# The last ConvFFN's seven-product down projection, regrouped: where its pieces are split, which queue loads its weights, and the order of its last steps

## The chip, the cores and the metric

The kernel runs on one core of one Trainium2 chip. Its engines are TensorE (PE; PEld is its weight load), VectorE (DVE), ScalarE (ACT), GpSimd (POOL) and SyncE (SP). Each works through its own instructions in order and waits for others at semaphores. Transfers are issued from the queues of SyncE, POOL and ScalarE and run on 16 DMA engines. The metric is device microseconds (us) of one execution, as the median of several runs.

## What is computed

One inference step of a two-layer encoder trunk with 1,024 prompt frames and 32 frames of a running stream, model width 1,024. Each layer has a recurrent mixer (retention in layer 0, gated linear attention in layer 1) and a convolutional feed-forward block. The change touches that block of layer 1 and the final norm:

```python
def conv_ffn(h, conv_state, w_up, conv_w, conv_b, w_down):
    u = h @ w_up
    T = u.shape[1]
    ext = jnp.concatenate([conv_state.astype(u.dtype), u], axis=1)
    c = conv_b + ext[:, 0:T] * conv_w[0]
    for j in range(1, CONV_W):
        c = c + ext[:, j:j + T] * conv_w[j]
    gate, val = jnp.split(c, 2, axis=-1)
    return (jax.nn.silu(gate) * val) @ w_down, ext[:, T:]
...
        y, cs = conv_ffn(h, conv_states[i], ffn_w_up[i], ffn_conv_w[i], ffn_conv_b[i], ffn_w_down[i])
        new_conv.append(cs)
        x = x + y
    return rmsnorm(x, norm_final), ...
```

The inner width is 2,816, so `u` has 5,632 columns. All data are float32.

## The kernel before

**Number format.** A float32 operand is split into a high part (`hi`, a ScalarE cast) and a low part (`lo`, a VectorE subtraction of the cast from the raw value). A product is then three matmuls: hi x hi, hi x lo, lo x hi.

**Tokens.** T = 1,056 columns (1,024 + 32) in four quarters of TH = 264. A "half" s = 0 or 1 is two quarters; one matmul covers one quarter's width of 264.

**Up stage (`ffn_up`).** 22 units f, each one 128-row tile of the gate half and one of the value half. A 2x2 block product is done with seven block products instead of eight (`seven`): sums of the activations (made once) and of the weights (per unit) are multiplied, and sums of the results taken. So a unit is 7 products x 2 halves, each product 4 x 3 matmuls. Results go from PSUM through ScalarE copies (`snap`, line 415) and VectorE additions (`put`, line 1818) to a buffer `U[f]`. When a unit is through, `conv(f)` makes the convolution of both tiles: per tile two POOL copies into `cst`, one ScalarE activation (line 1844) and two VectorE instructions (1845, 1846), then a SiLU and the gate product (1869, 1870). In layer 1 `pair_sums` goes on: two units make a pair k = f // 2, and seven sums of the pair's blocks (line 1866) are stored as seven pieces in `scr_h7`.

**Down stage (`Down7`).** 11 pairs k against 4 pairs p of output tiles, again seven products m = 1, 2, 6, 5, 7, 4, 3 (`ORD`). It runs in steps n = 0 to 13: step n takes pairs n-3 to n (those that exist) against output pair p = (n + 1) % 4, so a step sums 1, 2, 3, 4, ... 4, 3, 2, 1 pairs: 44 in all. A step has 7 products i x 2 halves s, each 3 matmuls per pair; steps 3 to 10 have 168 matmuls, all steps 1,848.

- `load_x(k, i)` loads a raw piece on SyncE into one of 28 regions (four pairs held at a time; pair k overwrites pair k - 4, which was last used in the step before) and returns `split`, the cast (1627) and the subtraction (1628). Pairs 0 and 1 are loaded during the last up unit (`early`). From pair 4 on, piece i of pair n + 1 is loaded behind product i of step n, and a piece is cast when the list `late` holds more than two.
- `weights(n)` loads two raw weight blocks, `dg` and `dv`, on SyncE (1637), and makes seven operands from them: three splits (1641, 1642), four sums (1647 to 1649, 1654) and the split of `dwv` (1651, 1652). There are three raw tiles and ten tiles for operands; a step uses seven. So a load must wait until an earlier raw tile has been read for the last time.
- `product` takes results out of PSUM: ScalarE copies m = 1 (1685), 6 (1689), 7 (1692); VectorE adds 2 (1687), 5 to 7's copy (1693), 4 (1695), 3 (1698). The bank of m = 5 is accumulated on by m = 3, the last product, which so has to wait for line 1693. Output blocks of 528 come from two rings, five blocks for A and two for B, and are added to the residual `scr_x` in memory by accumulating transfers on POOL (1702).
- From step 10 on `settle` adds the products to the residual itself, which `fetch` has loaded into `Y` (additions at 1713), `squares` sums squares per quarter, and when the last output pair is through, `rms_row` (two matmuls `pn` with ones, line 231, and short ScalarE and VectorE steps, 243 to 250) and the lines 1749 and 1753 normalise a quarter and store it.

**What sets the order.** The program text gives priorities; a scheduler then places every instruction in its engine's order, one whose inputs it thinks late behind others. Engines keep that order on the chip. `order(a, b)` makes the scheduler place a behind b without a semaphore.

```python
                    if 2 <= n + 1 < len(self.win) and i == (2 if n > 2 else 0):
                        self.weights(n + 1)
...
                    elif 3 < k < NP:
                        late.append(self.load_x(k, i))
                    if len(late) > 2 or late and k >= NP:
                        late.pop(0)()
```

## Time and profile before

| what | value |
|---|---|
| median of 3 runs | 2818.47 us (2817.72 to 2820.93) |
| the profiled execution's own time | 2821.19 us |
| its span, first to last instruction | 2819.4 us |
| mean granted TensorE clock | 0.993 |
| first matmul of the down stage | 2542.0 us |
| transfers in the whole run | 379.90 MB, 135 GB/s on average |

A profile is one execution. Its span leaves out what lies ahead of the first and behind the last instruction. A row of a group of instructions reads: line, engine, operation, what it writes and reads, shapes and count, then busy time and mean duration, then idle time of that engine just before, with what ended it. A row of waits reads: who waited at which line, for whom, then us in total, times and the longest. A row of transfers reads: what, queue, count, KB each, median us from issue to landing. Matmul durations overlap, so the work of TensorE is best counted by matmuls per time.

### The profile page before, as it was taken

What the parts mean: (1) busy time and instruction counts of PE and PEld (TensorE: products, weight loads), DVE (VectorE), ACT (ScalarE), POOL (GpSimd) and SP (SyncE); (2) the same over time, 40 slices, a digit from 0 to 9 for tenths busy, and PEclk for the clock granted to TensorE, in tenths of its full rate; (3) what the DMA queues carried; (4) which work ended last, traced back from release to release, by engine and by line L of the source; (5) the groups of instructions that cost most, each with busy time, mean ns of one, the idle gap of its engine ahead of it and who ended that gap; (6) DMA issues with size and microseconds to landing.
All of it is one profiled execution on the core that took longest, in us unless ns stands there. A gap on an engine that the chain in (4) does not pass through costs nothing.

```text
span 2819.4 us, 54440 instructions
## 1 busy us (share of the span) xinstructions
PE 2762.1 (98%) x21954; PEld 2670.4 (95%) x21954; DVE 1989.9 (71%) x3450; ACT 1349.7 (48%) x2475; POOL 344.5 (12%) x628
## 2 busy tenths in 40 slices
PE   9999999999999999999999999999999999998997
PEld 9999988888999999999999999999999999998986
DVE  7876666667457877777555576764478888888657
ACT  7544454444345444444444466653354444455434
POOL 0000000000122111111000132210131111111112
PEclk9999999999999999999999999999999999999998
DMA  6333455554875222223755411116532332348772
GB/s 238 96 110 105 149 147 148 139 145 133 279 240 176 76 86 75 84 76 102 255 184 172 154 35 47 53 53 217 173 108 95 100 106 88 107 131 212 196 210 89
DMA packets 236158, 379.90 MB, mean 135 GB/s; under 512 B 58560, under 2 KB 162624, under 8 KB 232064
## 3 DMA queue, kind: packets, MB, share of 16 engines
q1 hardware_dynamic: 222864, 328.33, 36.0%
q0 software_dynamic: 12496, 47.54, 6.5%
q8 instruction: 172, 2.82, 0.4%
q14 instruction: 82, 0.67, 0.1%
q10 hardware_dynamic: 544, 0.54, 0.1%
HBM read 264.68 MB, written 111.67 MB: 133 GB/s over the span
## 4 chain that ended last, share of the span: by engine, by line
PE 80%; DVE 7%; ACT 3%; DMA 3%; issue 3%; POOL 2%; SPq 0%; DVEq 0%; ACTq 0%; POOLq 0%
PE pu L441 13%; PE pu L436 13%; PE pu L440 13%; PE pd L1519 5%; PE pd L1521 5%; PE pd L1520 5%; PE psv L270 2%; PE psv L271 2%; PE psv L272 2%; POOL x L1122 2%; PE pu L1676 2%; PE pu L1678 2%; PE pu L1679 2%; DMA raw<-w_ro 1%; DMA XA<-scr_h 1%
## 5 line engine op out<-in xcount | busy, mean ns | idle before, releaser
L110 DVE TENSOR_TENSOR wlo<-raw,whi 128x1024 fp32r<-128x1024 f32 x131 | 163.1, 1249 | 130.6 <-ACT whi L110 122.7
L415 ACT COPY HR<-pu 128x264 f32<-128x264 f32 x264 | 98.8, 375 | 302.5 <-PE pu L441 296.5
L110 ACT CAST whi<-raw 128x1024 fp32r<-128x1024 f32 x131 | 136.9, 1049 | 176.0 <-PE pd L1520 110.1
L441 PE MATMUL pu<-XA,wgl 128*128 128x264 f32 x752 | 213.4, 284 | 0.0
L436 PE MATMUL pu<-XA,wgh 128*128 128x264 f32 x752 | 212.8, 283 | 0.1
L440 PE MATMUL pu<-XA,wgh 128*128 128x264 f32 x752 | 212.6, 283 | 0.0
L1845 DVE SCALAR_TENSOR_TENSOR AR<-AR,cw 128x1058 f32<-128x1058 f32 x88 | 115.7, 1317 | 72.9 <-ACT AR L1844 71.4
L1818 DVE TENSOR_TENSOR AR<-HR,pu 128x264 f32<-128x264 f32 (+2 forms) x440 | 144.3, 367 | 3.0 <-PE pu L441 2.8
L1520 PE MATMUL pd<-hl,whi 128*128 128x384 f32 (+1 forms) x440 | 142.2, 323 | 0.1
L1519 PE MATMUL pd<-hh,whi 128*128 128x384 f32 (+1 forms) x440 | 142.2, 323 | 0.0
L1521 PE MATMUL pd<-hh,wlo 128*128 128x384 f32 (+1 forms) x440 | 141.8, 322 | 0.0
L436 PEld LDWEIGHTS pu<-XA,wgh 128*128 128x128 f32 x752 | 141.2, 188 | 0.3 <-ACT wgh L372 0.3
L440 PEld LDWEIGHTS pu<-XA,wgh 128*128 128x128 f32 x752 | 141.2, 188 | 0.0
L441 PEld LDWEIGHTS pu<-XA,wgl 128*128 128x128 f32 x752 | 141.1, 188 | 0.0
L436 PE MATMUL pu<-XA,wsh 128*128 128x264 f32 x464 | 132.5, 286 | 1.8 <-ACT HR L415 0.7
L373 DVE TENSOR_TENSOR wtl<-rv,wth 128x1024 fp32r<-128x1024 f32 x58 | 71.0, 1224 | 88.3 <-ACT wth L372 88.3
L441 PE MATMUL pu<-XA,wtl 128*128 128x264 f32 x464 | 131.9, 284 | 0.0
L441 PE MATMUL pu<-XA,wsl 128*128 128x264 f32 x464 | 131.8, 284 | 0.0
L436 PE MATMUL pu<-XA,wth 128*128 128x264 f32 x464 | 131.6, 284 | 0.0
L440 PE MATMUL pu<-XA,wsh 128*128 128x264 f32 x464 | 131.4, 283 | 0.0
L440 PE MATMUL pu<-XA,wth 128*128 128x264 f32 x464 | 131.1, 283 | 0.0
L1519 PE MATMUL pd<-XH,whi 128*128 128x264 f32 x432 | 123.6, 286 | 0.0
(604 smaller groups left out, 10529.5 us busy)
## 6 DMA issues: line engine op xcount, KB each, us to landing
raw<-w_down SPq DMA_DIRECT2D x60, 512.0 KB, 3.6
rg<-w_up SPq DMA_DIRECT2D x44, 512.0 KB, 3.5
rv<-w_up SPq DMA_DIRECT2D x44, 512.0 KB, 3.5
scr_h<-AR SPq DMA_DIRECT2D x77, 264.0 KB, 2.6
raw<-w_ro SPq DMA_DIRECT2D x39, 512.0 KB, 5.6
XH<-scr_hr POOLq DMA_DIRECT2D x16, 1056.0 KB, 7.1
scr_x<-AR POOLq DMA_DIRECT2D x60, 264.0 KB, 6.0
scr_h<-AR SPq DMA_DIRECT2D x22, 512.0 KB, 2.6
```

What stands on the lines that cost most here:

```text
L110: ins = S.copy(hi, raw), V.tensor_tensor(lo, raw, hi.bitcast(F32), op=ALU.subtract)
L270: PE.matmul(ps, ah, hi, start=kt == 0, stop=False)
L373: split_end[0] = split_last[0] = V.tensor_tensor(l_, src, h.bitcast(F32), op=ALU.subtract)
L415: ins = S.copy(t, b)
L436: mm = PE.matmul(ps, wh[:, k], x[:, 0, kt], start=m in (1, 2, 4, 5) and kt == 0, stop=False, skip_group_check=True)
L440: PE.matmul(ps, wh[:, k], x[:, 1, kt], start=False, stop=False, skip_group_check=True)
L441: mm = PE.matmul(ps, wl[:, k], x[:, 0, kt], start=False, stop=kt == 3, skip_group_check=True)
L1519: PE.matmul(o, w[0][:, k], h[0][:, :n], start=i == 0, stop=False)
L1520: PE.matmul(o, w[0][:, k], h[1][:, :n], start=False, stop=False)
L1521: self.last_mm = PE.matmul(o, w[1][:, k], h[0][:, :n], start=False, stop=i == nk - 1)
L1818: last_put[0] = V.tensor_tensor(u[:, d:d + n], t[:, o:o + n], b[:, o:o + n], op=op)
L1845: V.scalar_tensor_tensor(cj, uj[:, 1:T + 3], cw[:, nt, 1:2], cj, op0=ALU.mult, op1=ALU.add)
```

## The change

- **Pairs 0 and 1 are split in the up stage.** In units 5 to 18 `ahead_split` loads one stored piece back, casts it, subtracts, and stores high and low half to a new scratch `scr_h2`. `load_x` then loads both halves, twice the bytes, and nothing is split for these pairs in the down stage.
- **Late pieces are cast later**: when `late` holds more than three, behind a product of half 1, and placed behind that product's last matmul by `order`.
- **Weights** of step 3 on are loaded on POOL's queue instead of SyncE's. Those of steps 12 and 13 get homes in regions that pair 7 has left.
- **The last convolution** (unit 21) with its pair sums is called at step 2, and its two sums at steps 3, instead of ahead of the down stage; `o_conv` and the table load go with it. The buffers move by 8 columns for it.
- **A third block** in ring B, where the pre-split buffer `ready` was.
- **Steps 11 to 13 by half**: all of half 0 first, then all of half 1; the loads of `Y` and of these weights move into step 10 and to the start of step 11.

```diff
@@ Down7.__init__
-            self.blocks = [[HR[:, o * b:o * b + b] for o in range(3)] + [AR[:, o * b:o * b + b] for o in (8, 9)],
-                           [AR[:, o * b:o * b + b] for o in (10, 11)]]
+            self.blocks = [[HR[:, o * b:o * b + b] for o in range(3)] + [AR[:, 8 + o * b:8 + o * b + b] for o in (8, 9)],
+                           [AR[:, o:o + b] for o in (8 + 10 * b, 8 + 11 * b, 6 * b + 4)]]
@@ Down7.load_x
+            if k < 2:
+                nc.sync.dma_start(v.rearrange("p m j u -> p m (j u)").bitcast(F32), io["scr_h2"][k, :, i:i + n])
+                return None
...
-            def split():
-                S.copy(hi, raw)
+            def split(behind=None):
+                ins = S.copy(hi, raw)
+                if behind is not None:
+                    order(ins, behind)
                 V.tensor_tensor(lo, raw, hi.bitcast(F32), op=ALU.subtract)
@@ Down7.weights
-        def weights(self, n):
+        def weights(self, n, home=None, queue=nc.sync):
...
-                nc.sync.dma_start(r[:, :2 * h], io["w_down7"][o:o + 2 * h * P].rearrange("(p c) -> p c", p=P))
+                queue.dma_start(r[:, :2 * h], io["w_down7"][o:o + 2 * h * P].rearrange("(p c) -> p c", p=P))
@@ Down7.run
-        def run(self):
...
+        def run(self, last_conv):
+            N = len(self.win)
+            seq = [(n, s, i) for n in range(NP) for i in range(7) for s in range(2)]
+            seq += [(n, s, i) for s in range(2) for n in range(NP, N) for i in range(7)]
+            late, todo = [], []
+            for n, s, i in seq:
+                self.product(n, s, i)
+                k = n + 1
+                if s == 0:
+                    if n < NP - 2 and k > 1 and i == (2 if n > 2 else 0):
+                        self.weights(k, None, G if n > 1 else nc.sync)
+                    if n == NP - 2 and i == 2:
+                        self.weights(k, None, G)
+                        self.fetch(3)
+                    if n == NP - 1 and i in (1, 4):
+                        self.weights(NP if i == 1 else NP + 2, None if i == 1 else self.at[21][0][:, 20 * TH:], G)
+                    if n == NP - 1 and i in (1, 3, 5):
+                        self.fetch(i // 2)
+                    if n == NP and i == 0:
+                        self.weights(NP + 1, self.at[24][0], G)
+                    continue
+                if n >= NP:
+                    continue
+                if n == 2 and i == 1:
+                    todo = last_conv()
+                if todo and n > 2 and i in (2, 5):
+                    todo.pop(0)()
...
+                elif 3 < k < NP:
+                    late.append(self.load_x(k, i))
+                if len(late) > 3 or late and k >= NP:
+                    late.pop(0)(self.ends[n, s, i])
@@ ffn_up
+        def ahead_split(n):
+            k, i = divmod(n, 7)
+            raw, hi = ready[:, 2 * TH:], ready[:, :2 * TH]
+            nc.sync.dma_start(raw, io["scr_h7"][k, :, i].rearrange("p s t -> p (s t)"))
+            S.copy(hi.bitcast(F32R), raw)
+            V.tensor_tensor(raw.bitcast(F32R), raw, hi, op=ALU.subtract)
+            nc.sync.dma_start(io["scr_h2"][k, :, i], ready)
...
+                if he is not None and 4 < f < 19 and (s, i) == (1, 2):
+                    ahead_split(f - 5)
...
-                if s == 1 and i == 6:
+                if s == 1 and i == 6 and (he is None or f < NF - 1):
                     conv(f)
-            later(sums_h, 2)
+            if he is None:
+                nc.sync.dma_start(io["o_conv"][l], cst)
+
+        def last_conv():
+            conv(NF - 1)
             nc.sync.dma_start(io["o_conv"][l], cst)
+            ln_exp_table(last_silu[0])
+            return sums_h
```

94 lines of the change are left out of this document (39 added, 55 removed).

## The prediction

> **What bounds the kernel now.** I read the page's engine line first, then busy time by stretch, then the waits of each queue in the stretch that the change rewrites.
>
> ```profile
> span 2819.4 us, 54440 instructions
> PE 2762.1 (98%) x21954; PEld 2670.4 (95%) x21954; DVE 1989.9 (71%) x3450; ACT 1349.7 (48%) x2475; POOL 344.5 (12%) x628
> ```
>
> TensorE bounds the whole; only places where it waits can give time back. Busy time by stretch (each engine's busy us, its instructions in brackets, then granted clock, DMA share and GB/s):
>
> ```profile
> core 0: us, PE busy (x) PEld busy (x) DVE busy (x) ACT busy (x) POOL busy (x), PEclk, DMA share, GB/s
> 2441.50:2541.50 100.00, 100.00 (x826) 100.00 (x825) 84.15 (x132) 51.42 (x74) 13.02 (x32) 1.00 0.40 131
> 2541.50:2610.00 68.50, 58.60 (x450) 56.69 (x450) 59.10 (x99) 34.62 (x60) 14.46 (x19) 0.98 0.81 209
> 2610.00:2742.00 132.00, 125.08 (x990) 123.40 (x989) 83.31 (x137) 55.52 (x101) 19.11 (x23) 0.98 0.77 202
> 2742.00:2764.00 22.00, 22.00 (x178) 22.00 (x178) 12.51 (x26) 7.46 (x16) 4.15 (x6) 0.98 0.60 137
> 2764.00:2796.00 32.00, 31.23 (x254) 30.81 (x252) 24.32 (x57) 19.04 (x48) 13.95 (x19) 1.00 0.02 6
> 2796.00:2819.40 23.40, 4.40 (x8) 1.80 (x8) 18.76 (x42) 6.47 (x17) 0.00 (x0) 0.54 0.55 186
> ```
>
> The first row is the end of the up stage: 826 products in 100 us, 0.121 us each, and TensorE never waits. At that price the down rows lose 68.5 - 450 x 0.121 = 14.0 us (steps n = 0 to 3), 132 - 990 x 0.121 = 12.1 (n = 4 to 9), 0.4 (n = 10) and 1.2 (n = 11 to 13); then come 23.4 us with almost no products. These 51 us are all that the change can win. Who waits, from 2541 on:
>
> ```profile
> ACT XA L1627 <- DMA XA<-scr_h: 63.9, 21, 5.4
> DVE XA L1628 <- ACT XA L1627: 31.2, 15, 6.0
> ...
> ACT AR L1692 <- DMA scr_x<-AR: 13.8, 4, 5.2
> ...
> DVE dv L1647 <- DMA dv<-w_down: 11.0, 5, 2.9
> ...
> PE pu L1676 <- DVE AR L1693: 9.5, 9, 2.1
> ```
>
> and of SyncE's own queue:
>
> ```profile
> SPq L1637 <- DVE dwsl L1642: 25.8, 7, 9.4
> ```
>
> (us in total, times, longest). This reads as one chain: on SyncE a weight load waits until VectorE has freed its raw tile; the piece loads queued behind it start late; ScalarE stands in a cast (L1627) whose data have not landed; VectorE stands in the subtraction behind that; the addition L1693 is queued behind the subtraction, and the last product of the step needs the bank that L1693 reads. The wait costs more than itself, because TensorE's clock is lower after it:
>
> ```profile
> 2736.50:2739.00 2.50, 0.71 (x6) 0.50 (x5) 1.93 (x4) 1.74 (x3) 0.00 (x0) 1.00 0.67 209
> 2739.00:2742.50 3.50, 3.47 (x18) 3.48 (x19) 3.35 (x7) 2.19 (x5) 0.94 (x2) 0.59 0.28 74
> ```
>
> After some 2 us without a product the granted clock is 0.59 for 3.5 us, 1.4 us more lost.
>
> **A: steps 0 to 3, -6 us.** The 14 pieces of pairs 0 and 1 are no longer split here, and the last convolution is put further back. The built order of VectorE shows, though, that its convolution instructions still stand inside steps 0 and 1, and its product in step 2. So VectorE, 59.1 of 68.5 us busy now, stays the bound here. I count its instructions in the changed order from the end of the up stage to the second L1693-type addition of step 2: 57. Durations (busy us and mean ns behind the first bar; a shape has one duration whatever its tile):
>
> ```profile
> L1628 DVE TENSOR_TENSOR XA<-XA 128x1056 fp32r<-128x1056 f32 x4 | 5.0, 1249 | 0.0
> L1628 DVE TENSOR_TENSOR XA<-XA 128x528 fp32r<-128x528 f32 x34 | 23.7, 704 | 31.3 <-ACT XA L1627 31.2
> L1642 DVE TENSOR_TENSOR dwtl<-dv,dwth 128x1024 fp32r<-128x1024 f32 x8 | 9.8, 1223 | 1.2 <-ACT dwth L1641 1.2
> L1642 DVE TENSOR_TENSOR dwtl<-dv,dwth 128x768 fp32r<-128x768 f32 x2 | 1.9, 954 | 0.1
> L1654 DVE TENSOR_TENSOR dv<-dv,dg 128x512 f32<-128x512 f32 x8 | 5.5, 690 | 0.2
> L1654 DVE TENSOR_TENSOR dv<-dv,dg 128x384 f32<-128x384 f32 x2 | 1.1, 555 | 0.0
> L1693 DVE TENSOR_TENSOR AR<-AR,pu 128x264 f32<-128x264 f32 x20 | 8.3, 422 | 0.8 <-ACT AR L1692 0.8
> L1845 DVE SCALAR_TENSOR_TENSOR AR<-AR,cw 128x1058 f32<-128x1058 f32 x2 | 2.6, 1314 | 0.0
> L1844 ACT ACTIVATE AR<-AR,cw 128x1058 f32<-128x1058 f32 x10 | 12.7, 1272 | 0.6 <-POOL cst L1842 0.5
> L1627 ACT CAST XA<-XA 128x528 fp32r<-128x528 f32 x32 | 20.3, 635 | 60.9 <-DMA XA<-scr_h 60.7
> ```
>
> Convolution 4 x 1.31; piece splits 4 x 1.25 + 2 x 0.70; weights of step 3 (3 x 1.22 + 5 x 0.69), of step 2 (3 x 0.96 + 5 x 0.55) and of step 1 (half of step 3's, with some overhead: 4.0); 20 additions at 0.42; the gate product 1.4: 38.2 us, less 0.07 where one instruction begins before the listed end of the last, 34. The changed TensorE order has 12 more up products ahead of the first down product (1.5 us); with one addition and the convolution's ScalarE part (1.27) VectorE starts at 2544.6 and is through at 2578.8. Now:
>
> ```profile
> 2587.83 0.76 DVE L1693 TENSOR_TENSOR AR<-AR,pu 128x264 f32<-128x264 f32 x2
> ```
>
> That is 9 us earlier if VectorE never idles; I allow it 3 us of waits and take 6. Ends: 0 (it waits as much as now, or the doubled loads are late) and 12 (of the 14.0).
>
> The doubled loads: pairs 0 and 1 now come from memory as high and low halves, 7.6 MB instead of 3.8, in the stretch where DMA stands at
>
> ```profile
> 2541.50:2551.50 10.00, 7.73 (x60) 7.18 (x59) 8.68 (x18) 6.83 (x13) 1.84 (x4) 1.00 0.93 314
> ```
>
> The first loads can go when the first up product of the last unit is done, 16 products of 12 x 0.121 us ahead of step 0, 23 us; with 1.6 MB of stores among them 9.2 MB at 314 GB/s take 29 us, so they end some 6 us into the down stage. Pair 1 is first needed at 42 x 0.121 = 5 us and its last piece at 14. The weights of step 1, queued behind them, land at about the time when VectorE's convolution lets their split run. I cost the loads at nothing beyond the 3 us; without that cover they cost up to 6.
>
> **B: steps 4 to 9, -8 us.** Each late piece is cast one step later, held behind a product, at least three products of both halves (3 x 2 x 12 x 0.121 = 8.7 us) after its load can start; weight loads leave SyncE for POOL, so a piece load waits for its region alone. Landing takes (KB each, median us; the last row is the whole run's):
>
> ```profile
> XA<-scr_h SPq DMA_DIRECT2D x32, 264.0 KB, 5.1
> dv<-w_down SPq DMA_DIRECT2D x8, 512.0 KB, 3.7
> scr_x<-AR POOLq DMA_DIRECT2D x28, 264.0 KB, 6.0
> XH<-scr_hr POOLq DMA_DIRECT2D x16, 1056.0 KB, 7.1
> ```
>
> 5.1 is under 8.7, so the cast waits go. The third output block takes away the 13.8 us in which L1692 waited for a store. What is late next is the dv load: in the changed order VectorE's first use of dv (L1647's like) stands two instructions behind the subtraction that frees its tile, and both additions that free banks stand behind it. That subtraction ends about 8 us into a step; with 0.9 us to issue (0.86 in the POOL row below) and 3.7 to 6.0 to land VectorE goes on at 13 to 15 us, and the additions are needed at 17.3 and 18.8. A subtraction and a 1.22 us weight split lie between, so it fits, with 0 to 3 us to spare. I take 8 of the 12.1, ends 0 and 12.
>
> The Trainium skill, "DMA: Bandwidth & Descriptors", section "Issuing engine by pattern", puts a plain load on Sync and calls that path generally faster, which speaks against this edit; the rows (3.7 on SyncE, 6.0 for half as much on POOL, though with accumulation) agree. Its section "Anatomy of one DMA — SWDGE (gpsimd) path" has 2.0 us plus bytes over 436e3: an estimate of 3.2 us for 512 KB, by which the spare would be kept and the sum unchanged; the rule as it stands leads to the second rival.
>
> **C: steps 10 to 13 and the end, -4 us.** Half s = 0 runs through steps 11 to 13 first, then s = 1, so two of four normalisations move beside products. From the chain of waits:
>
> ```profile
> 2797.83 1.26 PE pn L231 x2
> 2803.85 0.34 DVE rt L249
> 2807.88 0.34 DVE rt L249
> 2815.03 0.81 DVE AR L1753 x2
> ```
>
> One quarter costs VectorE 4.0 us (2803.85 to 2807.88); the last store takes from 2815.84 to 2819.4. Now 2764 to 2819.4 is 55.4 us. After: s = 0's products 126 x 0.121 = 15.2; TensorE then waits 2.2 for two squares and three additions ahead of the row sum, which all s = 1 products are queued behind; then VectorE, not TensorE, sets the pace: 0.6 + 8.0 for two quarters, and 21 additions and 4 square sums (18 x 0.42 + 3 x 0.70 + 4 x 0.42 less 25 x 0.07: 9.6, and 1.1 for ScalarE's squares between them), 19.3 against 15.2 of products; row sum and two quarters 9.3; store 3.6: 49.6. The weights of step 12 are requested only when their raw tile is free, with 1.6 us of VectorE work before their first use, which then waits some 3 us for POOL's load; half of it shows, 1.5. Gain 55.4 - 51.1 = 4, ends -1 (both waits in full) and 7.
>
> **D: up stage, +1 us.** Fourteen times a load, a cast (0.64, 635 ns above), a subtraction (0.70) and a store. VectorE goes from 84 to about 88 busy in 100, ScalarE has half its time free, and TensorE's only wait in this whole stage is
>
> ```profile
> PE pu L440 <- DVE XH L315: 0.6, 1, 0.6
> ```
>
> On SyncE the load is behind a weight load and the store waits for the subtraction, ahead of weight loads that are wanted a unit later. Ends 0 and the third rival.
>
> Sum: -6 - 8 - 4 + 1 = -17. The profiled execution took 2821.2 us (span 2819.4), 2.7 above the median of 2818.5; so 2804.2 for such an execution and **2801.5** for the median.
>
> **The rivals.**
> - All waits go: A 12, B 12, C 5, D 0: 2789.5. For it: every cause in the table of waits is addressed. Against: VectorE's 34 us in steps 0 to 2.
> - POOL's weight loads come late. POOL holds its fourth transfer back until an earlier one has landed:
>
> ```profile
> 2634.22 0.86 POOL L1702 DMA_DIRECT2D scr_x<-AR  x1 [3.32 <-issue]
> ```
>
>   With 3.3 us on top, dv lands at 16 to 18 us of a step, the additions come 1 to 3 us late in each of six steps, and B is gone: 2809.5.
> - Slower: the pre-split stalls the up stage. If VectorE stands in each of the 14 subtractions as in L1628 now (31.2 / 15 = 2.1 us) and a bank's addition is behind it, 14 x 2.1 = 29: 2801.5 + 29 - 1 = 2829.5. It is slower than before from 1.3 us a unit (18 / 14). Against: the subtraction stands far behind its cast in the order, and additions have no wait to show.
> - Steps 0 to 3 give nothing (doubled loads, VectorE idle): 2807.5.
> - The edits only move waits, A and B at 0 with C: 2815.5.
>
> **How the numbers follow.** Forecast 0.50 (its own range 2796 to 2807), all waits gone 0.12, POOL late 0.15, steps 0 to 3 nothing 0.10, moved waits 0.06, slower 0.07. Two measurements of this kernel can tell about 0.2%, 5.6 us: faster means under 2812.9. The first four make 0.87; I take 0.84, as the fourth and second can meet; same 0.08, slower 0.08. The range 2790 to 2813 leaves out the last two and part of the first rival.
>
> **What would show it.** Right: no SyncE row with a weight load waiting in the down stage, cast waits under 15 us in all (now 63.9 for XA), under 8 us lost in each of A and B by the count of products, VectorE busy without a break in the end, the up stage still at 826 products in 100 us. Wrong: VectorE waiting for dv more than 11 us, TensorE waits in the up stage, or a last product that leaves more than 13 us behind it.

## The result, and the profile after

The changed kernel takes **2812.01 us** in the median of 7 executions (2805.3 to 2814.6) against 2818.47 us before (7 executions beside it, 2816.8 to 2820.9): a ratio of **0.9971, 95% interval 0.9960 to 0.9983**. In a second session it was 2806.89 us against 2820.06, a ratio of 0.9959 (0.9945 to 0.9974). So it is faster, by 6 to 13 us between medians (less than half a per cent), and not by the 17 of the forecast. Its executions spread over 9.3 us in both sessions, those of before over 4.1 (7 executions) and 13.2 (15).

From the page of the changed kernel, its span and its engine line:

```profile
span 2805.6 us, 54515 instructions
...
PE 2757.1 (98%) x21954; PEld 2666.6 (95%) x21954; DVE 1990.9 (71%) x3456; ACT 1353.8 (48%) x2481; POOL 363.3 (13%) x650
```

The profiled execution took 2807.3 us, 4.7 less than the median of its kernel; the one of before took 2.7 more than its own. Two profiles side by side therefore show 7 us more than two medians, and what is read from them is read by stretch. Line numbers have moved: the cast of a piece is now 1630, its subtraction 1633, the weight loads 1642, the first sum on `dv` 1660, the product's lines 1689 to 1712 (the addition that frees a bank, 1693 before, is 1707), the store to the residual 1716, the load of residual rows 1721, `settle` 1727, the squares 1749 to 1754. In the kernels without the pre-split these numbers are two or three lower.

Busy time by stretch (length, each engine's busy us with its instructions in brackets, granted clock, DMA share, GB/s), 100 us of the up stage, steps 0 to 3, steps 4 to 9, half 0 of steps 11 to 13, half 1, and the rest:

```profile
2440.00:2540.00 100.00, 100.00 (x826) 100.00 (x825) 80.66 (x128) 43.79 (x66) 14.57 (x32) 1.00 0.40 137
...
2542.50:2603.00 60.50, 53.93 (x423) 52.00 (x423) 51.86 (x86) 33.64 (x57) 16.79 (x23) 1.00 0.93 264
2603.00:2728.80 125.80, 123.17 (x1010) 122.75 (x1009) 83.45 (x138) 57.77 (x102) 27.59 (x37) 1.00 0.83 217
...
2749.30:2772.10 22.80, 18.61 (x134) 17.02 (x133) 14.56 (x34) 13.51 (x34) 8.49 (x11) 0.96 0.01 1
2772.10:2792.10 20.00, 17.32 (x128) 16.40 (x127) 17.94 (x40) 9.25 (x23) 7.17 (x8) 0.93 0.32 109
2792.10:2805.60 13.50, 1.57 (x4) 0.50 (x2) 8.09 (x17) 2.54 (x6) 0.00 (x0) 0.50 0.48 161
```

By the prediction's count of products, steps 0 to 3 still lose 60.5 - 423 x 0.121 = 9.3 us, steps 4 to 9 only 125.8 - 1010 x 0.121 = 3.6, and the end holds 13.5 us with four matmuls. DMA is busy 0.93 of the time in steps 0 to 3, and VectorE stands idle for 8.6 of 60.5 us there, about as long as before (9.4 of 68.5). The DMA share alone does not show that data come late: the faster kernel `no_presplit` below has 0.92. What shows it are the landing times of `no_presplit` and the changed kernel, side by side below.

Who waits, from 2541 us on, and then the waits of SyncE's own queue (us in total, times, longest):

```profile
DVE dv L1660 <- DMA dv<-w_down: 35.7, 11, 6.7
...
ACT XA L1630 <- DMA XA<-scr_h: 9.9, 3, 5.2
...
PE pu L1689 <- DVE AR L1707: 4.6, 4, 2.3
```

```profile
SPq L1721 <- DMA scr_x<-AR: 18.5, 4, 7.8
...
SPq L1642 <- DVE dwsl L1655: 9.1, 1, 9.1
...
SPq L1721 <- DMA scr_x<-HR: 6.7, 2, 5.6
```

The XA casts wait 9.9 us where they waited 63.9, and only one weight load still waits on SyncE (step 2's, which did not move). What is left on that queue is the 1 MB load of residual rows (1721), which stands there until an addition on POOL has landed, 25.2 us in all, with piece loads behind it. It did so before as well (30.3 us from step 5 to step 10), in the shadow of the weight loads.

To compare stretches between executions I cut every profile at three marks: the first product of the layer-1 up stage, the first product of step 5 (up to there the order of TensorE mixes steps), and the first product of step 11. The changed kernel by these stretches (the first number behind the marks is the length):

```profile
2090.30:2623.40 533.10, 525.51 (x4290) 522.27 (x4289) 455.42 (x707) 261.79 (x395) 92.88 (x189) 1.00 0.47 151
2623.40:2749.30 125.90, 123.27 (x1011) 122.85 (x1010) 86.10 (x151) 57.96 (x107) 26.83 (x36) 1.00 0.80 208
2749.30:2805.60 56.30, 37.49 (x262) 33.92 (x260) 40.59 (x89) 25.30 (x62) 15.66 (x19) 0.84 0.23 78
```

Before, by the same marks:

```profile
2091.20:2629.10 537.90, 526.98 (x4291) 523.62 (x4290) 455.99 (x704) 260.67 (x390) 85.04 (x178) 1.00 0.40 121
2629.10:2764.00 134.90, 127.98 (x1010) 126.30 (x1009) 82.54 (x140) 54.22 (x101) 21.07 (x25) 0.97 0.74 194
2764.00:2819.40 55.40, 35.62 (x262) 32.61 (x260) 43.08 (x98) 25.51 (x65) 13.95 (x19) 0.80 0.24 82
```

The up stage with steps 0 to 4 gained 4.8 us, steps 5 to 10 gained 9.0, the end lost 0.9. These stretches begin one step later than the forecast's terms (A: steps 0 to 3, B: steps 4 to 9); by the count of products above, A gained 14.0 - 9.3 = 4.7 us and B 12.1 - 3.6 = 8.5, which is nearly the same. The up stage's start itself lies anywhere from 2087.3 to 2092.3 in the profiles of this study, whatever was changed behind it, and is left out of every comparison of stretches below.

### The profile page after: what moved, and what is told of

The parts are those of the page before. It is cut to its first block, busy times and chain, and to the rows that moved or that the text cites. A ratio compares the mean times of both kernels' runs of the same rounds, so it can differ in the third digit from the quotient of the medians.

```text
span 2805.6 us, 54515 instructions
## 1 busy us (share of the span) xinstructions
PE 2757.1 (98%) x21954; PEld 2666.6 (95%) x21954; DVE 1990.9 (71%) x3456; ACT 1353.8 (48%) x2481; POOL 363.3 (13%) x650
## 4 chain that ended last, share of the span: by engine, by line
PE 81%; DVE 7%; ACT 3%; issue 3%; POOL 3%; DMA 2%; SPq 0%; DVEq 0%; POOLq 0%; ACTq 0%
PE pu L441 13%; PE pu L436 13%; PE pu L440 13%; PE pd L1519 5%; PE pd L1521 5%; PE pd L1520 5%; PE psv L270 2%; PE psv L271 2%; PE psv L272 2%; POOL x L1122 2%; PE pu L1689 2%; PE pu L1691 1%; PE pu L1692 1%; PE pg L133 1%; PE pg L134 1%
## 5 line engine op out<-in xcount | busy, mean ns | idle before, releaser
L1519 PE MATMUL pd<-XH,whi 128*128 128x264 f32 x432 | 123.5, 286 | 0.0
```

The source lines that it names most:

```text
L1519: PE.matmul(o, w[0][:, k], h[0][:, :n], start=i == 0, stop=False)
```

## The experiments

There were fifteen runs: fourteen other kernels, and the changed one a second time. "Plain" stands for the changed kernel without the pre-split of pairs 0 and 1 (`no_presplit`). Stretches are those of the three marks, from one profile each; median and ratio are from 4 to 10 executions with runs of the kernel before on the same chip beside them. The median of before lay between 2818.5 and 2821.0 us in these sessions, so the ratio compares best.

| kernel | median us | ratio to before (95%) | to step 5 | steps 5 to 10 | end |
|---|---|---|---|---|---|
| before (its profile) | 2818.5 | 1 | 537.9 | 134.9 | 55.4 |
| after (its profile) | 2812.0 | 0.9971 (0.9960 to 0.9983) | 533.1 | 125.9 | 56.3 |
| after_again | 2806.9 | 0.9959 (0.9945 to 0.9974) | 534.6 | 127.5 | 56.1 |
| c_inter | 2808.6 | 0.9956 (0.9940 to 0.9971) | 534.5 | 130.2 | 55.6 |
| w_sync | 2808.8 | 0.9967 (0.9956 to 0.9978) | 531.0 | 129.0 | 56.9 |
| w_ahead | 2806.9 | 0.9947 (0.9934 to 0.9959) | 533.1 | 125.4 | 56.4 |
| no_presplit ("plain") | 2797.5 | 0.9922 (0.9909 to 0.9936) | 527.1 | 123.2 | 55.2 |
| np_double | 2807.2 | 0.9953 (0.9940 to 0.9966) | 534.2 | 123.8 | 56.2 |
| np_upsplit | 2796.9 | 0.9917 (0.9904 to 0.9931) | 528.7 | 123.4 | 55.4 |
| np_order | 2799.0 | 0.9927 (0.9913 to 0.9940) | 527.9 | 123.5 | 56.2 |
| np_inter | 2800.2 | 0.9932 (0.9919 to 0.9946) | 527.6 | 124.1 | 55.8 |
| np_mix | 2799.1 | 0.9921 (0.9908 to 0.9934) | 526.4 | 123.9 | 57.6 |
| np_conv | 2805.0 | 0.9944 (0.9931 to 0.9957) | 532.9 | 123.0 | 56.0 |
| np_late2 | 2804.5 | 0.9940 (0.9926 to 0.9954) | 527.2 | 130.8 | 56.3 |
| np_wsync | 2807.2 | 0.9956 (0.9943 to 0.9969) | 529.2 | 133.1 | 55.2 |
| np_fetch | 2804.6 | 0.9942 (0.9929 to 0.9954) | 528.4 | 129.0 | 55.3 |
| np_blk2 | 2806.7 | 0.9954 (0.9940 to 0.9968) | 528.7 | 137.1 | 56.3 |

### The changed kernel once more (`after_again`)

No edit.

> The changed kernel itself, for a second profiled execution. The first one took 2807.3 us, the median of seven was 2812.0, with 2805.3 to 2814.6 between them. Theory of the spread: what differs between executions lies in steps 4 to 9, where piece loads on SyncE and weight loads on POOL now run at one time; a second execution that takes 2810 or more then shows steps 4 to 9 longer than the 125.9 us of the first, by about the difference in the total, and the last part (from step 11 on) again 56 +- 0.7 us. Rival: steps 4 to 9 are steady (126 +- 1 us) and the difference lies in steps 0 to 3, in the last part or ahead of the down stage. Median 2812 +- 2 under both.

2806.9 us (2804.9 to 2814.2); the profiled execution, at 2809.4, was 2.0 us above the first one. Of its stretches the first is 1.5 longer, steps 5 to 10 are 1.6 longer, the end is 0.2 shorter. So neither theory holds alone: the two executions differ ahead of step 5 and in steps 5 to 10, not in the end. The largest single wait, at the end of step 7, is 2.6 us in the first profile and 3.6 in this one.

### The last steps in the old order (`c_inter`)

```diff
-            seq = [(n, s, i) for n in range(NP) for i in range(7) for s in range(2)]
-            seq += [(n, s, i) for s in range(2) for n in range(NP, N) for i in range(7)]
+            seq = [(n, s, i) for n in range(N) for i in range(7) for s in range(2)]
```

> The changed kernel with the last three steps in the old order, both token halves in turn. Theory: the new order gave nothing, since the first half's part stretched (from step 11 to the end 56.3 us against 55.4 before); the last part is 55 to 56 us and the median within 1 us of 2812 or up to 2 us under it. Rival, the prediction's term C: the new order is worth 4 us, and without it the median is 2816.

2808.6 us, within what the changed kernel itself shows, and the end takes 55.6 us. By the end's length the order by half is worth nothing here; nothing of term C is seen.

### The weights back on SyncE (`w_sync`)

All four places give `nc.sync` for `G`.

```diff
-                        self.weights(k, None, G if n > 1 else nc.sync)
+                        self.weights(k)
```

> The changed kernel with all weight loads of the down stage back on SyncE's queue. If POOL's queue for the weights carries the gain of steps 4 to 9 (9.1 us in the profiled execution), the waits of SyncE for a raw tile come back (some 25 us in all), the XA casts wait over 30 us, and the median is 2817 to 2821. Rival: the later cast and the third block carry it; median 2810 to 2813, and with pieces and weights one behind the other the executions lie closer together than the 9.3 us of the changed kernel.

2808.8 us, 1.2 under the rival's 2810 to 2813 and far from 2817; the spread is 10.3 us, so the rival was wrong about that. With the pre-split in place the queue makes no difference that can be seen in the median. By stretch it does: steps 5 to 10 are 1.5 to 3.1 us longer than in the two profiles of the changed kernel, and what lies ahead of step 5 is 2.1 to 3.6 shorter. `np_wsync` below takes up the first of these.

### No pre-split (`no_presplit`)

`load_x` loses its branch for k < 2, `early` appends and runs the splits as it did before, nine of them are run ahead of the first product, and `ahead_split` is not called.

```diff
-            if k < 2:
-                nc.sync.dma_start(v.rearrange("p m j u -> p m (j u)").bitcast(F32), io["scr_h2"][k, :, i:i + n])
-                return None
...
+                if (n, s, i) == (0, 0, 0):
+                    later(self.splits, 9)
                 self.product(n, s, i)
...
-                if he is not None and 4 < f < 19 and (s, i) == (1, 2):
-                    ahead_split(f - 5)
```

> The changed kernel with pairs 0 and 1 loaded raw and split at the start of the down stage, as before, and no pre-split in the up stage. Prediction's terms A and D: steps 0 to 3 go from 60.4 us back to about 66, the up stage gains 0 to 1, median 2816 to 2818. Rival: what the pre-split saves VectorE is given back by doubled loads; steps 0 to 3 stay within 2 us of 60.4 and the median within 2 us of 2812.

Neither: **2797.5 us**, 9 to 15 us *faster* than with the pre-split, 22 us faster than before. Steps 0 to 3 did not go back to 66 us, they lost their waits, and in steps 5 to 10 TensorE is now busy all but 0.2 us:

```profile
2615.50:2738.70 123.20, 122.99 (x1011) 122.78 (x1009) 86.31 (x152) 58.01 (x107) 28.25 (x38) 1.00 0.82 215
```

and the stretch that in the changed kernel is steps 0 to 3:

```profile
2542.50:2603.00 60.50, 60.09 (x489) 59.54 (x488) 58.82 (x98) 34.97 (x61) 17.64 (x24) 1.00 0.92 229
```

489 products where the changed kernel makes 423, with VectorE busy 58.8 of 60.5 us instead of 51.9. VectorE also has splits of pairs 0 and 1 to do and gets further, since what it needs is there. Where the difference comes from is seen in the transfers of the 42 us around the start of the down stage (all transfers, then groups: queue, count, KB each, median us to landing). The changed kernel, 2518 to 2560 us:

```profile
DMA packets 5278, 14.28 MB, mean 340 GB/s; under 512 B 431, under 2 KB 1967, under 8 KB 4507
...
XB<-scr_h SPq DMA_DIRECT2D x3, 528.0 KB, 11.3
...
dg<-w_down SPq DMA_DIRECT2D x1, 256.0 KB, 9.3
```

Plain, 2516 to 2558 us:

```profile
DMA packets 6768, 11.97 MB, mean 285 GB/s; under 512 B 493, under 2 KB 2157, under 8 KB 6765
...
XB<-scr_h SPq DMA_DIRECT2D x3, 528.0 KB, 5.5
...
dg<-w_down SPq DMA_DIRECT2D x1, 256.0 KB, 4.3
```

The same transfers, raw pieces (in XB) and the smaller weight block, take twice as long to land behind the doubled bytes.

### The bytes alone, the up stage alone, the place in the queue alone

`np_double` is plain, with each raw piece of pairs 0 and 1 loaded twice:

```diff
             nc.sync.dma_start(raw, io["scr_h7"][k, :, i:i + n].rearrange("p m s t -> p m (s t)"))
+            if k < 2:
+                nc.sync.dma_start(hi.bitcast(F32), io["scr_h7"][k, :, i:i + n].rearrange("p m s t -> p m (s t)"))
```

> The changed kernel without the pre-split (2797.5 us), but each raw load of pairs 0 and 1 is made twice, into the high and the low half, so that as many bytes come in at the start of the down stage as with the pre-split, while VectorE splits as before. Theory: the doubled bytes, and the weights of steps 1 to 3 queued behind them, cost the 10 to 14 us by which the pre-split is slower; the median is 2806 to 2814 and steps 0 to 3 take 60 us or more. Rival: the loads cost nothing (as the prediction had it) and the loss comes from the up stage or from a changed order of VectorE; the median stays within 2 us of 2797.5.

2807.2 us: the loss is back in full. 7.1 us of it lie ahead of step 5, 0.6 in steps 5 to 10, 1.0 in the end. But in this kernel's built order the weights of step 1 stand behind all pieces of pairs 0 and 1, in plain their first block stands behind three loads. The next three are to tell bytes from place.

`np_upsplit` is plain, with `ahead_split` called as in the changed kernel and its stored halves not read:

> The changed kernel without the pre-split, to which the 14 loads, casts, subtractions and stores in the up stage are added back, their result unused: the prediction's term D alone. Prediction: +1 us (2798.5), the up stage still 826 products in 100 us. Rival: the stores and the waits on SyncE's queue carry part of the 10 to 14 us; 2801 or more.

2796.9 us, 0.6 under plain. Term D cannot be told from nothing; the prediction had 1.

`np_order` is plain, with step 1's weight loads held behind the piece loads issued so far:

```diff
-                queue.dma_start(r[:, :2 * h], io["w_down7"][o:o + 2 * h * P].rearrange("(p c) -> p c", p=P))
+                ins = queue.dma_start(r[:, :2 * h], io["w_down7"][o:o + 2 * h * P].rearrange("(p c) -> p c", p=P))
+                if n == 1:
+                    order(ins, self.last_load)
```

> The changed kernel without the pre-split, where the weight loads of step 1 are put behind the piece loads of pair 1 on SyncE's queue, as the pre-split has them; the bytes stay as they are (3.8 MB of pieces). If it is the place in the queue that cost np_double its 10 us, the median is 2803 to 2808; if it is the bytes, it stays within 2 us of 2797.5.

2799.0 us, 1.4 over plain: the place costs little while the bytes are few.

`w_ahead` is the changed kernel, with the raw loads of step 1's weights called at product 3 of the last up unit and their splits left where they were:

```diff
+            if (s, i) == (0, 3):
+                self.first = self.raws(1)
             if (s, i) == (1, 5):
-                self.weights(1)
+                self.weights(1, raws=self.first)
```

> The changed kernel, pre-split and doubled bytes kept, but the weights of step 1 are loaded after four of the pieces of pair 0 and not behind all of pairs 0 and 1. Place in the queue: 2797 to 2801. Bytes: 2806 to 2812, and the pieces of pair 3, which now land at 2564 to 2567 us in the changed kernel, still land after 2555.

2806.9 us. The waits for step 1's weights are gone, but the last pieces of pair 3 now land at 2569 and 2571 us, 17 us after they are issued, and TensorE stands still for 2.7 us up to 2562.9 and 3.9 up to 2573.1 instead. Whatever is put first, something else is late.

`np_double`, `np_upsplit` and `np_order` together say that it is the bytes, not the up stage and not the place of step 1's weights. One other place was not tried by itself. In the changed kernel, in `np_double` and in `w_ahead` the scheduler put step 2's `dv` load, which waits 5.5 to 9.1 us on SyncE for its raw tile, ahead of the last pieces of pair 3; in plain and `np_order` it stands behind them. In `np_double` 6.3 of the 7.1 us are lost by the 126th matmul of the down stage, before pair 3 is needed, which speaks for the bytes. In the changed kernel 2.1 us are lost by then and 5.2 by the 252nd matmul, where step 3 and with it pair 3 begins, so there this place may have a part.

### The load of residual rows (`np_fetch`)

```diff
-            nc.sync.dma_start(self.Y[p], scr_x[:, 2 * p:2 * p + 2])
+            order(nc.sync.dma_start(self.Y[p], scr_x[:, 2 * p:2 * p + 2]), self.last_load)
```

In the text of the kernel the first of these loads stands in step 9. The scheduler places it two steps earlier, as soon as it thinks the row final, ahead of three piece loads that are due. What this does in the changed kernel's step 7 is read from POOL's timeline (start, length, what, idle before and what ended it):

```profile
2661.29 0.56 POOL L1642 DMA_DIRECT2D dg<-w_down  x1 [8.23 <-DVE AR L1707]
2661.97 1.78 POOL L1716 DMA_DIRECT2D scr_x<-AR  x2
2663.89 0.84 POOL L1716 DMA_DIRECT2D scr_x<-HR  x1
2669.36 0.86 POOL L1716 DMA_DIRECT2D scr_x<-AR  x1 [4.63 <-DVE XH L1633]
```

from SyncE's waits in these 28 us, and from the chain of waits:

```profile
SPq L1721 <- DMA scr_x<-HR: 5.6, 1, 5.6
SPq L1721 <- DMA scr_x<-AR: 1.9, 1, 1.9
```

```profile
2674.59 7.91 DMA XA<-scr_h
...
2685.28 0.43 DVE AR L1707
```

POOL stands at the weight load until a raw tile is free; the additions behind it then go together, and the fourth goes at 2669.4, when the first, issued at 2661.97, has landed at 2669.05. SyncE stands 7.5 us at the residual row, until that fourth addition has landed at 2674.0. The piece load behind it is issued at 2674.6, next to the row's 1 MB, and needs 7.9 us. Its cast, a cast and a subtraction of weights and the addition that frees the bank follow, and TensorE goes on at 2685.8 after 2.6 us.

> The changed kernel without the pre-split, where the four 1 MB loads of the residual rows are held behind the last piece load issued before them, so that no piece load stands behind a load that waits for an addition on POOL's queue. Theory: in steps 7 to 10 that queue cost the changed kernel its largest wait (2.6 to 3.9 us in three profiles) and costs 0.5 to 1 us here; median 2795 to 2797. Rival: the last loads come late for step 10 and the last part; 2798 to 2803.

2804.6 us, 1.6 over the rival's range, by the rival's mechanism. In its profile steps 5 to 8 run without any wait of TensorE (81.8 us for four steps, 20.45 each); but the row of step 10 now comes late, and TensorE stands 4.1 us at 2746. 3.3 us of the difference in its profile lie ahead of the up stage. There was little to win in step 7: in plain the load stands at the same place and SyncE waits 6.8 us there, but the step takes 20.96 us, 0.5 more than here. So what the load's place does to TensorE in the changed kernel (step 7: 23.0 us) is read from the chain of waits and not shown by this run, and the place further back is no remedy.

### What carries steps 4 to 9: the later cast, the weights' queue, the third block

`np_late2`, plain, with `len(late) > 2` for `> 3`; SyncE's order is the same as plain's:

> The changed kernel without the pre-split, its late pieces cast one product earlier (two products after their load instead of three), a part of the prediction's term B. If the later cast carries B, the XA casts wait 20 us more in steps 4 to 9 and the median is 2802 or more; if 5.8 us (two products) are enough for a load that lands in 5 us, it stays within 2 us of 2797.5.

2804.5 us, steps 5 to 10 7.6 us longer. The waits of the XA casts in these steps (us, times, longest), in plain and in `np_late2` (where the cast's line is 1627):

```profile
ACT XA L1627 <- DMA XA<-scr_h: 6.9, 3, 3.6
```

```profile
ACT XA L1627 <- DMA XA<-scr_h: 22.1, 10, 9.9
```

15 us more of cast waits go with 7.6 us more of these steps. 5.1 of them lie in step 7 and 2.5 in step 9, where piece loads stand behind the residual row: two products' time is too little for a load that stands behind a waiting one.

`np_wsync`, plain with the four edits of `w_sync`:

> The changed kernel without the pre-split and with all weight loads of the down stage on SyncE's queue. Prediction's term B: the piece loads wait behind weight loads that wait for a raw tile; steps 5 to 10 go from 123.2 us to 128 or more and the median to 2802 or more. Rival (with the pre-split the queue made no difference): within 2 us of 2797.5.

2807.2 us, steps 5 to 10 9.9 us longer. SyncE's weight loads wait again:

```profile
SPq L1639 <- DVE AR L1704: 12.1, 5, 6.2
SPq L1639 <- DVE XB L1652: 6.6, 1, 6.6
```

8.2 of the 9.9 us lie in steps 9 and 10, where the two longest of these waits are. So POOL's queue is worth as much as the whole of term B once the start is not short of data. The Trainium skill, "DMA: Bandwidth & Descriptors", section "Issuing engine by pattern", would have a plain load on Sync. Here the measurement decides against it (2807.2 us on SyncE's queue, 2797.5 on POOL's). From step 3 on the 512 KB `dg` loads take 4.6 us on POOL's queue in plain and 3.6 on SyncE's in `np_wsync`, the `dv` loads 5.3 and 5.7; what decides is which loads have to stand behind them.

`np_blk2`, plain with two blocks in ring B:

```diff
-                           [AR[:, o:o + b] for o in (8 + 10 * b, 8 + 11 * b, 6 * b + 4)]]
+                           [AR[:, o:o + b] for o in (8 + 10 * b, 8 + 11 * b)]]
```

> The changed kernel without the pre-split and with two output blocks in the second ring instead of three. If the third block carries part of term B, ScalarE's copies wait again for the stores (13.8 us before) and the median is 2800 to 2806; rival: with the queues changed the store of two steps ago has long landed, and it stays within 2 us of 2797.5.

2806.7 us, but not by the wait that the expectation named. ScalarE waits for a store only 2.5 us, ahead of step 5 (at 2571.9 and 2593.2 us). The 13.8 us before also lay there, in steps 1 and 2 (2566.8 to 2583.6 us), so the third block was never part of term B. The loss is in steps 5 to 10, 13.9 us. The scheduler moved the second residual load six piece loads forward, and in step 8 the chain of waits runs there: a store issued at 2688.1 lands 4.45 us later, the residual load goes, the piece load behind it takes 7.89 us from 2693.2; then cast, weights, addition follow; TensorE waits 2.1 us, and 2.8 and 3.7 at the same place of the steps on both sides, where the residual loads did not move. What the third block is worth by itself stays open.

### The last convolution (`np_conv`)

Plain, with the last convolution, its sums and the table load at the end of the up stage as before.

```diff
-                if s == 1 and i == 6 and (he is None or f < NF - 1):
+                if s == 1 and i == 6:
```

> The changed kernel without the pre-split and with the last convolution back at the end of the up stage, a part of the prediction's term A. If the late convolution carries what steps 0 to 4 gained (from the first up product to step 5 527.1 us, 537.9 before), the median is 2804 to 2808; rival: the gain of these steps comes from the third block and the queue; within 2 us of 2797.5.

2805.0 us; in the profile all of it lies ahead of step 5 (532.9 against 527.1). Who makes TensorE wait between 2540 us and step 5 (us, times, longest):

```profile
PE pu L1686 <- ACT HR L1700: 2.6, 1, 2.6
PE pu L1686 <- ACT HR L1696: 1.6, 1, 1.6
PE pu L1686 <- ACT AR L1703: 1.4, 2, 0.8
```

These are ScalarE's copies out of banks, which plain shows with 0.2 us in all; I read them as late because ScalarE is at the convolution. For the longest its timeline bears that out: the copy starts at 2554.5 us, right behind the SiLU of the convolution (1.13 us from 2552.1) and the table load (1.28 us). The late convolution is worth some 6 us.

### The order of the last steps (`np_inter`, `np_mix`)

`np_inter` is plain with the edit of `c_inter`:

> The changed kernel without the pre-split and with the last three steps in the old order (both token halves in turn), the prediction's term C where executions lie close together. Theory: the new order is worth nothing (last part 55.2 us against 55.4 before); median within 1.5 us of 2797.5. Prediction: it is worth 4 us; 2801.5.

2800.2 us, between the two, and its ratio's interval overlaps plain's; of its 2.6 us only 0.6 lie in the end, the rest in stretches that the edit does not touch.

`np_mix` puts the half's handover behind products of the other half:

```diff
-            seq += [(n, s, i) for s in range(2) for n in range(NP, N) for i in range(7)]
+            seq += [(n, 0, i) for n in (NP, NP + 1) for i in range(7)] + [(NP, 1, i) for i in range(3)]
+            seq += [(NP + 2, 0, i) for i in range(7)] + [(NP, 1, i) for i in range(3, 7)]
+            seq += [(n, 1, i) for n in (NP + 1, NP + 2) for i in range(7)]
...
+                if (n, s, i) in ((NP, 1, 5), (NP + 1, 1, 0)):
+                    self.rows.pop(0)()
```

> The changed kernel without the pre-split, with the last three steps in a third order: the first half's steps 11 and 12, three products of the second half's step 11, the first half's step 13, then the rest of the second half; the first half's two row sums stand 3 and 5 products later, behind products of the second half. Theory of the term C: the 3.5 us in which TensorE waits for the squares at the handover, and the 1.5 us ahead of the last product of the first half, gave back what the new order won; hidden, the part from step 11 to the end is 51 to 53 us (55.2 now) and the median 2793.5 to 2796. Rival: VectorE paces the whole part, as the prediction had it for the second half alone, and the time only moves behind the last product; 55 us and 2797 to 2799.

2799.1 us, near the rival, though the end takes 57.6 us and not 55. The handover is hidden, and the time comes back behind it. Busy time by stretch in `np_mix`:

```profile
2760.00:2769.30 9.30, 9.30 (x72) 8.88 (x71) 8.69 (x18) 7.36 (x19) 4.23 (x5) 1.00 0.06 18
2769.30:2776.00 6.70, 1.78 (x13) 1.35 (x11) 6.61 (x16) 0.00 (x0) 0.00 (x0) 0.86 0.64 216
```

TensorE makes 72 products without a break around the handover, where plain made 8 in the 3.6 us from 2757.0, and then 13 in 6.7 us, while VectorE is busy 6.6 of them with the two normalisations. The granted clock then is 0.50 from 2774.2 us to the end; in plain it falls only at 2781.3.

## Why the prediction was right and wrong, step by step

**The way to read it** held: TensorE bounds the whole, the up stage kept 826 products in 100 us, and every gain came out of waits in the down stage. The sign held, the median of 2812.0 lies at the edge of the range, and the size was wrong: 6.5 us came of the 17.

**A, -6, with D, +1: -4.8 came, by two errors that cancel,** so the figure is luck. The step that failed is "I cost the loads at nothing beyond the 3 us; without that cover they cost up to 6". The runs put the doubled loads at about 10 us: 2807.2 for the bytes alone against 2797.5, of which 7.1 lie ahead of step 5 (6.0 between the changed kernel and plain). They run into the down stage as foreseen; of what is queued behind them I had looked at step 1's weights alone, and those took 9.3 us to land where plain has 4.3 and 5.8. I left out the weights of step 2 and the raw pieces of pairs 2 and 3, which took from 0.4 to 5.8 us longer each; the last piece of pair 3 landed at 2566.8 us, in plain at 2550.5. The other error is "VectorE ... stays the bound here" as a reason for a small gain. In plain VectorE is as good as full in these 60.5 us (58.8 busy), but TensorE is fuller (60.1) and hardly waits, and 10.8 us are gained ahead of step 5, near the upper end of 12: VectorE's work fits beside the products if it is never kept waiting. Of those, some 6 are the late convolution's (`np_conv`).

**B, -8: -9.0 came,** for two of the three reasons given. Cast waits for XA fell to 9.9, below the 15 named, and the steps lost 3.6. `np_late2` and `np_wsync` take back 7.6 and 9.9 of the 11.7 us that plain gains in steps 5 to 10, so the later cast and the queue are both needed. The third reason fails: the 13.8 us in which ScalarE waited for a store lie in steps 1 and 2, in A's stretch. "What is late next is the dv load" was wrong where it matters: VectorE waits 35.7 us for dv, three times the mark of 11 at which I would have called the step wrong, and TensorE hardly notices. In plain, with 24.6 us of it in steps 5 to 10, those steps take 123.2 us, 6 x 168 x 0.121 = 122.0 being their products. What is late next is the piece load behind the residual row, a load that waited on the same queue before and that I had not followed, since the diff moves only the place from which it is called.

**C, -4: +0.9 came,** the other step that failed: "s = 0's products 126 x 0.121 = 15.2; TensorE then waits 2.2", 17.4 us. The half took 22.2, from 2749.3 to 2771.5, and these 4.8 us are nearly all of the miss: the second half took 19.9 up to its row sum (19.3 in the sum), and from there to the end 14.2 (12.9); the 1.5 for late weights did not show. The first half's waits, the last of them up to the handover:

```profile
2751.30:2753.20 1.90, 0.33 (x3) 0.12 (x1) 1.87 (x4) 1.73 (x4) 1.54 (x2) 1.00 0.00 0
...
2766.40:2768.20 1.80, 0.32 (x4) 0.10 (x2) 1.54 (x4) 1.05 (x4) 1.14 (x2) 1.00 0.00 0
2768.20:2769.70 1.50, 0.64 (x4) 0.43 (x4) 1.05 (x3) 1.11 (x3) 0.34 (x1) 1.00 0.00 0
2769.70:2772.10 2.40, 2.14 (x6) 1.38 (x7) 1.41 (x4) 1.45 (x5) 0.00 (x0) 0.59 0.00 0
```

I had let VectorE pace the second half alone. In the first half no engine is full (VectorE is busy 14.6 of 22.8), but TensorE waits twice for a chain of short steps, a `settle` addition, squares on ScalarE, their sum on POOL, the next addition (the rows at 2751.3 and 2766.4, 1.6 and 1.5 us without products), and 2.8 us pass from the end of the half's last product (2768.7) to the next half's first (2771.5), row sums included. What the products gain by covering two normalisations is lost again in these waits. `np_mix` shows that it cannot be had by order alone: with the handover hidden, VectorE's work comes due in one piece behind it. The rival of waits that only move had them in A and B; it is C for which it holds.

**From the sum to the median.** By stretch the profiles give -4.8 - 9.0 + 0.9 = -12.9, where the forecast's terms made -17; C is the difference. The medians give -6.5 and, in the second session, -13.2. I had taken the median of the changed kernel to lie 2.7 under its profiled execution, as before's does. That step failed too: the changed kernel's executions differ by 9.3 us, and the one profiled first was among its fastest. The forecast for the profiled execution missed by 3.1 us (2804.2, measured 2807.3), that for the median by 10.5 (2801.5, measured 2812.0); the 7.4 between them are 2.7 and the 4.7 by which the profiled execution lies under its median. So of the 10.5, 7.4 are this step's and 3.1 the sum's, where C, 4.9 too much, weighs most. Why executions differ stays open. The doubled loads are not needed for it: plain's five lie within 3.3 us, but those of `np_late2` and `np_wsync`, which have no doubled loads, within 9.9 and 10.7, and before's within 13.2 in the second session.

**The rivals.** "Steps 0 to 3 give nothing" (2807.5) named the doubled loads as its reason and comes nearest to the mechanism, though these steps did give 4.8 of the 10.8 us that they could. "POOL's weight loads come late" has its mechanism in the traces (POOL stands 12.2 us at a `dg` load, and additions go late behind it), and its 2809.5 is the nearest figure to 2812.0, by luck: it hits the residual row on SyncE and not VectorE. The slower one, pre-split stalls in the up stage, is out: `np_upsplit` is at plain's time.

**A better version** is plain: 2797.5 us, 0.9922 of before (0.9909 to 0.9936), which beats both. It is the change with a part left out that the forecast had in its second largest term.

## What to carry to other kernels

Work taken off one engine by moving twice the bytes is only free where the transfers behind it are not wanted soon: list every load queued after the doubled ones, with the time at which its consumer needs it, before you put the price at nothing. A load that has to wait for a store stalls its whole queue, so read the built order of that queue, not the text. And when one stretch has slack on every engine, a reordering of it is paid in chains of short dependent steps, which a sum of busy times does not show.

## What the hardware did that was not expected

**One wait's length does not decide the clock.** The prediction read, from one place, that some 2 us without products lower the granted clock. The changed kernel's longest wait in steps 5 to 10, 2.6 us without products up to 2685.8 us, left it at 1.00. A wait of 3.6 us in `np_late2`, with what follows:

```profile
2674.05:2677.60 3.55, 0.28 (x3) 0.07 (x1) 1.06 (x3) 1.72 (x4) 0.00 (x0) 1.00 0.56 203
2677.60:2679.20 1.60, 1.55 (x12) 1.53 (x12) 1.51 (x2) 1.60 (x4) 0.00 (x0) 1.00 0.02 7
2679.20:2682.60 3.40, 2.91 (x14) 2.68 (x13) 2.31 (x6) 1.36 (x2) 2.53 (x4) 0.50 0.40 106
```

and one of 3.9 us in `c_inter`:

```profile
2685.60:2689.40 3.80, 0.24 (x2) 0.02 (x1) 2.25 (x4) 3.15 (x5) 0.00 (x0) 0.88 0.20 78
2689.40:2691.40 2.00, 1.92 (x8) 1.93 (x9) 1.66 (x5) 0.71 (x2) 1.77 (x3) 0.50 0.33 59
```

The clock falls 1.6 us behind the end of the first wait and inside the second; it stays at 0.50 for 3.41 us in `np_late2` and for 6.83 in `c_inter`. At 0.50 eight products are made in 2 us, where the changed kernel made fifteen at 1.00 (2685.7 to 2687.7 us): 0.8 us lost in the 2 us shown. Two waits that differ by 0.3 us can differ by more than that in what they cost. The Trainium skill, "TensorE: Matmul & The Clock Gate", section "Part 1: The HAM clock gate (the "warmup" mystery)", tells of a window of about 3.4 us that runs freely, so that its place counts. The traces agree: in every profile with more than one fall from 2520 us on, the falls lie whole multiples of 3.41 us apart (before: 40, 13 and 17 of them). Laid on that grid, the wait of 2.1 us that the prediction quotes falls into one window, and the longer one of the changed kernel is divided between two (11 matmuls begin in the first of these rows, 16 and 20 in the last two; the rows also count those that reach into them):

```profile
2736.25:2739.66 3.41, 1.60 (x13) 1.39 (x13) 2.69 (x5) 2.40 (x5) 0.00 (x0) 1.00 0.57 183
2739.66:2743.07 3.41, 3.41 (x17) 3.41 (x17) 3.31 (x7) 1.53 (x3) 1.51 (x3) 0.50 0.53 87
```

```profile
2681.36:2684.77 3.41, 2.12 (x18) 1.91 (x16) 1.34 (x2) 2.25 (x4) 0.00 (x0) 1.00 0.40 132
2684.77:2688.19 3.42, 2.43 (x20) 2.44 (x21) 3.29 (x7) 2.25 (x4) 2.27 (x4) 1.00 0.34 73
```

Some 28 products of 0.121 us fit into a window. Of the windows between 2540 and 2765 us that began at full clock, in all 17 profiles, the 9 in which at most 8 matmuls began were all followed by a fall, 9 of the 13 with 9 to 12, and none of the 1,079 with 13 or more.

**POOL's fourth accumulating transfer waits for the first.** In every burst of four from 2540 to 2765 us in the changed kernel, `np_blk2` and `np_late2` the fourth addition of a burst was issued 0.31 us after the first had landed (2669.36 after 2669.05, 2693.09 after 2692.78, 2713.34 after 2713.03 in the changed kernel), whatever the wait table names as its cause. A burst of four therefore takes two landing times, 12 us in step 7 (2661.97 to 2674.04), and whoever waits for the last waits for both.

**Landing times double under load.** The 528 KB pieces in XB took 5.5 us in plain and 11.3 behind the doubled loads, at 285 and 340 GB/s on average over the 42 us; the pieces in XH took 17.1 in `w_ahead`. The median of 5.1 us for 264 KB, on which term B rested, was taken over the whole down stage and is no price for these 42 us.
